# A partner step, two fetches, the spills and the two score lanes put elsewhere in a hybrid decoder layer

## The chip, the cores and the metric

The kernel runs on one core of one Trainium2 chip. The metric is the device time of one execution in microseconds (us); the median of three runs is compared. The engines are TensorE (PE, matmuls), VectorE (DVE), ScalarE (ACT), GpSimd (POOL) and SyncE (SP). SP and POOL here mostly issue DMAs, each in the order of its own program. Every engine works through its program in order and waits at an instruction until the semaphores it needs have been raised.

## The reference

One layer over 256 tokens of width 2048, in float32:

```
h = rmsnorm(x, pre_norm_g);  proj = h @ w_in          # w_in: 2048 x 18448, split into 11 parts
gk  = log_sigmoid(a_lr @ gla_gk_w2 + gla_gk_b) / 16
o_a = gated linear attention(a_q, a_k, a_v, gk)        # 4 heads, keys 256, values 512
y_a = (rmsnorm(o_a) * silu(a_g)) @ w_branch_a
o_b = (softmax(q1 k1) - lam * softmax(q2 k2)) v        # 16 heads, causal, key width 64
y_b = (rmsnorm(o_b) * 0.8 * silu(b_g)) @ w_branch_b
merged = sigmoid(m_a) * y_a + sigmoid(m_b) * y_b
out = x + rmsnorm(merged @ w_out, post_norm_g)
```

## The kernel before

Every weight is read once (some twice) from DRAM as float32 and split into two parts, `hi` and `lo`: ACT copies it rounded (L261), DVE subtracts (L262). A product is then three matmuls, hi x hi, hi x lo and lo x hi. A piece of weights of 128 x 1024 is a *half step*; `take` hands the next one to PE and has the one three places ahead prepared (`AHEAD = 3`; three buffers each for `hi` and `lo`, so ACT waits until PE has let one go).

The work has these stages.

1. The first projections with the values of the linear attention. Beside them, tasks written as generators go forward a piece at each `pump`: `forget_gate` works out the forget gate (absolute value, exponential and logarithm on ACT, last a combination on DVE), `sum_operands` prepares sums of the input's blocks (`s4`, `r1`, `s2`, `r3`).
2. The joint phase. Seven *sets* of 1024 columns are done with seven block products each, by a scheme that needs one product fewer than eight (`PRODUCTS = (1, 3, 5, 6, 2, 7, 4)`). Products 1, 6, 7 and 4 of a set share one PSUM bank `x`: DVE reads it after 6 and after 7 (`gr`, L765 and L773), ACT after 4. So product 4's first matmul waits until DVE has read the bank. A product is two *slots* (t = 0, 1) of two half steps. `phase_steps` mixes the slots with the other projections: behind a slot stands a *partner*, a half step of `others()` (16 matmuls in a `bg` bank), except behind the slots in the list `skip`. There are 14 slots without a partner. In this phase PE's order is the program's (`pinned`).
3. The lanes. `gla_scores` and `gla_out` do the linear attention, two `diff_lane` generators the softmax attention, each in its turn at each `pump`, while the main loop projects the gates, the last heads and `y0`. `q` and `k` of the linear attention were spilled to DRAM and are fetched back (`fetched`) on POOL's queue. A lane's round for a pair of heads is: turned output of the last pair and scores of the first head; scores of the second; turn the first (L1021, evacuated by ACT L1023); weigh the first (L1032 to L1034) and turn the second; weigh the second.
4. `y1`, the merge, the output projection and the norm.

There are eight PSUM banks: four of tag `mm` for main work and four of tag `bg` for everything beside it. Main work and tasks share `take`'s stream of weights. `fetch` keeps its DMA in program order; `spill` leaves it to the scheduler, which may move it among what stands near. Names after `<-` are operands; `raw` is a weight piece as loaded, `a`, `b`, `c` are the sets' weight pieces, which are partly added up by the DMA itself (`accumulate`).

Of the kernel before, what the change touches and what calls it, by code (L numbers as in the profile page):

```python
# [29 lines left out]
SETS = 7  # L30
# [46 lines left out]
def phase_steps():  # L77

    keys = ["v4"] + [f"{name}{hf}{c}" for hf in range(2) for name in ("k", "q") for c in range(4)]
    keys += [f"{name}{g}{c}" for g in EARLY for pair in range(2) for name in ("dq", "dk") for c in (2 * pair, 2 * pair + 1)]  # L80
    other = [(key, r, h) for key in keys for r in range(4 if key == "v4" else 1) for h in range(2)]
    slots = [(s, prod, t) for s in range(SETS) for prod in PRODUCTS for t in range(2)]
    front = [(0, prod, t) for prod in PRODUCTS[:2] for t in range(2)]
    skip = [(SETS - 1, 7, 1), (SETS - 1, 4, 1)] + [(s, prod, 0) for prod in (4, 2) for s in range(SETS - 1, 0, -1)]
    skip = skip[: len(slots) + len(front) - len(other)]
    mixed = []
    for slot in slots:
        mixed += [("set", *slot, h) for h in range(2)]
        for _ in range((slot not in skip) + (slot in front)):
            mixed.append(other.pop(0))  # L90
    return mixed + other
# [3 lines left out]
def hybrid_kernel(ctx: ExitStack, tc, xt, xn, preg, postg, w, w2, gkb, glag, lamv, diffg, ident_d, causal_d, lmask_d, out):  # L95
    nc = tc.nc
    pe, act, dve, pool, sp = nc.tensor, nc.scalar, nc.vector, nc.gpsimd, nc.sync
# [12 lines left out]
    def u(shape, name, dtype=F32):  # L110
        count[0] += 1
        return big.tile(shape, dtype, tag="u", name=f"{name}_{count[0]}")
# [5 lines left out]
    def sm(shape, name, dtype=F32, bufs=2):  # L118
        count[0] += 1
        return pools[0].tile(shape, dtype, tag=name, name=f"{name}_{count[0]}", bufs=bufs)  # L120

    def t2(shape, name):
        count[0] += 1
        return pools[0].tile(shape, F32, tag="t2", name=f"{name}_{count[0]}", bufs=6 if len(pools) == 1 else 12)

    def spill(t, name):
        count[0] += 1
        d = dram.tile(list(t.shape), t.dtype, name=f"{name}_{count[0]}")
        pool.dma_start(d, t)
        return d  # L130

    def fetch(d, name, make, queue=pool):
        t = make(list(d.shape), name, d.dtype)
        tc.keep_in_program_order(queue.dma_start(t, d))
        return t

    def ps(tag):
        count[0] += 1
        return psum.tile([P, 512], F32, tag=tag, name=f"{tag}_{count[0]}")

    def f32(ap):
        return ap.bitcast(F32)
# [370 lines left out]
    def lend(tag, name, dtype=F32):  # L513

        count[0] += 1
        return blocks.tile([P, 8, P], dtype, tag=tag, name=f"{name}_{count[0]}", bufs=1).rearrange("p a t -> p (a t)")

    def forget_gate():
        w2_raw = w2_tile[0]
        yield  # L520
        bank = ps("bg")
        for b in range(2):
            pe.transpose(bank[:, P * b : P * b + P], lr[:, b, :], ident)
        top = t2([P, 512], "lrh").bitcast(F32R)
        lrt = sm([P, S], "lrt", F32R, bufs=1)
        act.activation(top[:, :S], bank[:, :S], AF.Copy)
        for i in (0, 64):
            act.activation(lrt[i : i + 32, :], bank[i : i + 32, :S], AF.Copy)
            r = slice(i + 32, i + 64)
            dve.tensor_tensor(out=lrt[r, :], in0=bank[r, :S], in1=f32(top[r, :S]), op=ALU.subtract)  # L530
        w2_s = lend("s2l", "w2_s", F32R)
        top = lend("r3h", "w2h", F32R)
        r = slice(64, P)
        late = tc.keep_in_program_order
        late(act.activation(w2_s[:64, :], w2_raw[:64, :], AF.Copy))
        late(act.activation(top[r, :], w2_raw[r, :], AF.Copy))
        late(dve.tensor_tensor(out=w2_s[r, :], in0=w2_raw[r, :], in1=f32(top[r, :]), op=ALU.subtract))
        yield
        gp.extend(u([P, 2, 4, P], "gp") for _ in range(2))
        for hf in range(2):  # L540
            for c in range(2):
                bank = ps("bg")
                for i in range(2):
                    ct = 4 * hf + 2 * c + i
                    o = bank[:, S * i : S * i + S]
                    pe.matmul(o, w2_s[:, P * ct : P * ct + P], lrt, start=True, stop=True)
                for i in range(2):
                    ct = 4 * hf + 2 * c + i
                    act.activation(gp[hf][:, :, 2 * c + i, :], bank[:, S * i : S * i + S].rearrange("p (b t) -> p b t", b=2), AF.Identity, bias=gkb_s[:, ct : ct + 1])
            yield  # L550
        e = [lend(tag, "e") for tag in ("r3h", "r3l")]
        z = [t.rearrange("p b c t -> p (b c t)") for t in gp]
        for hf in range(2):
            act.activation(e[hf], z[hf], AF.Abs)
            yield
            act.activation(e[hf], e[hf], AF.Exp, scale=-1.0)
            yield
        for hf in range(2):
            act.activation(e[hf], e[hf], AF.Ln, bias=1.0)
        for hf in range(2):  # L560
            yield
            dve.scalar_tensor_tensor(out=z[hf], in0=z[hf], scalar=0.0, in1=e[hf], op0=ALU.min, op1=ALU.subtract)
        done.add("gate")
# [71 lines left out]
    def late():  # L635
        norm_row()
        yield
        lam()
        yield
# [143 lines left out]
    pinned[0] = True  # L783
    fetched = []
    for step in phase_steps():
        if step == ("set", SETS - 1, 4, 0, 0):
            fetched = [[fetch(ts[name, hf], name, u) for name in ("q", "k")] for hf in range(2)]
        next(sets if step[0] == "set" else rest)
    for gen in (sets, rest):
# [160 lines left out]
    def place(t, d, m, h):  # L950
        tc.keep_in_program_order(sp.dma_start(f32(t[64 * h : 64 * h + 64, m]), d[64 * m : 64 * m + 64]))

    waiting = [(g, pair) for g in range(4) for pair in range(2)]

    def diff_lane(n):
# [11 lines left out]
        def ask():  # L967
            if waiting:
                ahead.append(waiting.pop(0))
                missing.extend(("q", "kh", "kl"))  # L970

        def arrive():
            if not missing or (*ahead[0], "dk") not in heads:
                return
            g, pair = ahead[0]
            part = missing.pop(0)
            for m in range(2):
                for h in range(2):
                    if part == "q":
                        place(q2, heads[g, pair, "dq"][h != m], m, h)  # L980
                    elif part == "kh":
                        place(kh, heads[g, pair, "dk"][0], m, h)
                    elif h == m:
                        place(kl, heads[g, pair, "dk"][1], m, h)
# [24 lines left out]
        def combine(w):  # L1009
            z, prob = w["z"], w["prob"]  # L1010
            c = sm([P, 2], "c", bufs=2)
            dve.reciprocal(out=c, in_=z[:, 2:4])
            dve.scalar_tensor_tensor(out=c, in0=z[:, 0:2], scalar=neg_lam, in1=c, op0=ALU.mult, op1=ALU.mult)
            for b in range(2):
                lo, up = cuts[b]
                dve.scalar_tensor_tensor(out=prob[0][:, lo:up], in0=prob[1][:, lo:up], scalar=c[:, b : b + 1], in1=prob[0][:, lo:up], op0=ALU.mult, op1=ALU.add)
# [46 lines left out]
        while ahead:  # L1063
            late = len(missing)
            while missing:
                arrive()
                yield
            if late:
                yield
            g, pair = ahead.pop()  # L1070
            one, two = (dict(g=g, h=2 * pair + i) for i in range(2))
            if last:
                turned_out(*last)
            last = g, pair
            scores(one)
            if g not in values:
                values[g] = [fetch(gspill[2 * g + 4 + i], name, u, sp) for i, name in enumerate(("dv", "ub"))]
            yield
            combine(one)
            scores(two)  # L1080
            yield
            ask()
            for work in (((turned, one), (combine, two)), ((weighted, one), (turned, two)), ((weighted, two),)):
                arrive()
                for part, w in work:
                    part(w)
                yield
# [6 lines left out]
    for g in range(4):  # L1094
        banks = token_major(f"ag{g}", 512, x_ops, LANES)
        t = u2([P, 2, 512], "ua")
# [62 lines left out]
    for g in range(4):  # L1159
        banks = token_major(f"y1{g}", 512, b_ops, 1 if g else LANES, None if g else settle)  # L1160
        for b in range(2):
            t = gb[g][:, b, :]
# [11 lines left out]
    for b in range(2):  # L1174
        xres.append([])
        for i in range(2):
            t = u([P, 1024], "xres")
# [126 lines left out]
```

## Time and profile before

| | |
|---|---|
| median of 3 runs | 1108.43 us (1108.39 to 1108.62) |
| profiled execution | 1108.06 us, span 1106.3 us, mean granted PE clock 0.997 |
| busy in the span | PE 1092.8 us, DVE 863.2, ACT 680.3, POOL 132.1 |
| DMA | 274.57 MB, mean 248 GB/s |

The span runs from the first to the last instruction; the time includes what lies around it. The profile's rows are start and length in us, engine, line, operation, `out<-in`, shape and count; behind them in brackets the idle time of the engine just before and what ended it. A "busy" PE need not be PE at its peak, since matmuls overlap: one of 512 columns shows 0.39 us, and the next starts after 0.23. So the spacing of starts tells the pace. In lists of waits the columns are total us, times, longest.

The joint phase lies between about 82 and 594 us, the lanes between 594 and 908, `y1` and the merge until about 1014.

### The profile page before, as it was taken

The page shows a single profiled execution, that of the slowest core. Times are in us where ns is not written, and L with a number is a line of the kernel's source. Part 1 is how long each engine was busy: PE and PEld are TensorE (multiplying, and loading weights), DVE is VectorE, ACT ScalarE, POOL GpSimd, SP SyncE. Part 2 cuts the span into 40 slices and gives each one's busy share as a digit, 9 for nine tenths or more (in the row PEclk, how much of TensorE's full clock was granted, in tenths as well). Part 3 has the DMA queues.
Part 4 walks back from the last instruction along what each step waited for, and adds up shares of the span by engine and source line. Part 5 has one row for each costly group of instructions (what it writes and reads, how often), then busy time and mean ns, then how long its engine had stood idle before and what let it go on. Part 6 is the DMA issues. An engine that isn't in the chain of part 4 may idle for free.

```text
span 1106.3 us, 15250 instructions
## 1 busy us (share of the span) xinstructions
PE 1092.8 (99%) x5522; PEld 939.0 (85%) x5522; DVE 863.2 (78%) x1200; ACT 680.3 (61%) x989; POOL 132.1 (12%) x201
## 2 busy tenths in 40 slices
PE   9999999999999999999999999999999999999997
PEld 8999888888888888888887888889888888888886
DVE  7797987979979889798898988668877764655463
ACT  7886766666667667667675555567776653444460
POOL 0201111121021210211212100121110110000000
PEclk9999999999999999999999999999999999999999
DMA  9869979699798897997957654697898666556752
GB/s 346 297 229 326 281 260 312 157 303 300 269 312 218 307 244 248 320 241 276 298 143 276 238 186 153 204 326 262 255 277 270 215 227 211 190 190 220 270 195 76
DMA packets 58268, 274.57 MB, mean 248 GB/s; under 512 B 7824, under 2 KB 9360, under 8 KB 39248
## 3 DMA queue, kind: packets, MB, share of 16 engines
q1 hardware_dynamic: 36192, 184.18, 47.7%
q0 software_dynamic: 20992, 88.09, 28.8%
q10 hardware_dynamic: 1008, 1.32, 0.4%
q8 instruction: 43, 0.70, 0.3%
q14 instruction: 33, 0.27, 0.1%
HBM read 248.40 MB, written 25.17 MB: 247 GB/s over the span
## 4 chain that ended last, share of the span: by engine, by line
PE 97%; DVE 1%; issue 1%; DMA 0%; ACT 0%; DVEq 0%; SPq 0%; POOLq 0%; POOL 0%; ACTq 0%
PE mm L449 65%; PE bg L449 22%; PE bg L437 2%; PE mm L422 2%; PE mm L437 2%; PE bg L862 1%; PE bg L422 1%; PE bg L996 1%; PE bg L997 1%; DMA raw<-in_w_dram 0%; PE bg L1021 0%; PE bg L1034 0%; PE bg L1033 0%; PE bg L1032 0%; PE bg L1153 0%
## 5 line engine op out<-in xcount | busy, mean ns | idle before, releaser
L261 ACT ACTIVATE hi<-raw 128x1024 fp32r<-128x1024 f32 (+3 forms) x275 | 282.6, 1031 | 285.1 <-PE mm L449 175.3
L262 DVE TENSOR_TENSOR lo<-raw,hi 128x1024 fp32r<-128x1024 f32 (+3 forms) x275 | 325.9, 1187 | 147.7 <-ACT hi L261 144.4
L449 PE MATMUL mm<-hi,xs 128*128 128x512 f32 (+1 forms) x848 | 215.6, 389 | 2.2 <-DVE gr L773 1.8
L449 PEld LDWEIGHTS mm<-hi,xs 128*128 128x128 f32 x848 | 157.7, 189 | 29.0 <-issue 2.2
L449 PE MATMUL bg<-xs,hi 128*128 128x512 f32 x640 | 164.9, 390 | 0.0
L262 DVE TENSOR_TENSOR lo<-a,hi 128x1024 fp32r<-128x1024 f32 x112 | 135.2, 1221 | 10.5 <-ACT hi L261 9.3
L449 PEld LDWEIGHTS bg<-xs,hi 128*128 128x128 f32 x640 | 120.4, 188 | 23.3
L261 ACT ACTIVATE hi<-a 128x1024 fp32r<-128x1024 f32 x112 | 118.7, 1060 | 28.2 <-PE mm L449 22.0
L449 PE MATMUL mm<-lo,xs 128*128 128x512 f32 (+1 forms) x424 | 118.5, 385 | 0.1
L449 PEld LDWEIGHTS bg<-xs,lo 128*128 128x128 f32 x640 | 87.3, 191 | 6.2
L449 PEld LDWEIGHTS mm<-lo,xs 128*128 128x128 f32 x424 | 79.7, 189 | 14.9 <-DVE lo L262 0.4
L449 PE MATMUL bg<-xs,lo 128*128 128x256 f32 x640 | 89.3, 283 | 0.0
L262 DVE TENSOR_TENSOR lo<-b,hi 128x1024 fp32r<-128x1024 f32 x56 | 67.5, 1223 | 8.5 <-ACT hi L261 7.6
L261 ACT ACTIVATE hi<-b 128x1024 fp32r<-128x1024 f32 x56 | 59.3, 1061 | 18.5 <-PE mm L449 16.5
L449 PE MATMUL mm<-hi,oah 128*128 128x512 f32 x128 | 50.9, 398 | 0.0
L449 PE MATMUL mm<-hi,obh 128*128 128x512 f32 x128 | 50.4, 394 | 0.0
L449 PE MATMUL mm<-hi,oal 128*128 128x512 f32 x128 | 50.1, 391 | 0.0
L449 PE MATMUL mm<-hi,obl 128*128 128x512 f32 x128 | 49.9, 390 | 0.0
L1007 ACT ACTIVATE prob<-prob,mx,score_scale 128x128 f32<-128x128 f32 x64 | 34.2, 536 | 13.3 <-DVE mx L1002 13.1
L449 PE MATMUL mm<-hi,mh 128*128 128x512 f32 x96 | 37.5, 390 | 0.0
L449 PE MATMUL mm<-hi,ml 128*128 128x512 f32 x96 | 37.4, 390 | 0.0
L198 POOL DMA_DIRECT2D b<-in_w_dram x28 | 24.3, 868 | 108.8 <-DVE a L206 98.4
(288 smaller groups left out, 1874.5 us busy)
## 6 DMA issues: line engine op xcount, KB each, us to landing
raw<-in_w_dram SPq DMA_DIRECT2D x120, 1024.0 KB, 5.6
a<-in_w_dram POOLq DMA_DIRECT2D x28, 512.0 KB, 13.8
c<-in_w_dram SPq DMA_DIRECT2D x28, 512.0 KB, 8.8
b<-in_w_dram POOLq DMA_DIRECT2D x28, 512.0 KB, 7.9
a<-in_w_dram POOLq DMA_DIRECT2D x12, 1024.0 KB, 5.3
b<-in_w_dram POOLq DMA_DIRECT2D x12, 1024.0 KB, 7.9
raw<-in_w_dram SPq DMA_DIRECT2D x14, 832.0 KB, 7.2
dh<-dh POOLq DMA_DIRECT2D x16, 256.0 KB, 4.3
```

Source lines behind the costliest of these rows:

```text
L198: pool.dma_start(chain[s, name, i][:, c], weights(f"set{s}", 2 + i)[0][:, c], accum_op=ALU.add)
L261: act.activation(hi_t[:, a:b], r[:, a:b], AF.Copy)
L262: dve.tensor_tensor(out=lo_t[:, a:b], in0=r[:, a:b], in1=f32(hi_t[:, a:b]), op=ALU.subtract)
L422: i = pe.matmul(out, lhs, rhs, start=first and n == 0, stop=last and n == len(pairs) - 1)
L437: i = pe.matmul(banks[g][b][:, :n], a[part][:, P * b : P * b + P], w[:, n * g : n * g + n], start=first, stop=last)
L449: i = pe.matmul(*args, **kw)
L862: pe.matmul(o, xk[:, P * c : P * c + P], xq.rearrange("p (b c t) -> p b c t", b=2, c=4)[:, :, c, :], start=i == 0, stop=i == 1)
L996: pe.matmul(banks[m][:, lo:up], q2[:, m, i2, t], kh[:, m, i2, :n], start=True, stop=False)
L997: pe.matmul(banks[m][:, lo:up], q2[:, m, i2, t], kl[:, m, i2, :n], start=False, stop=True)
L1007: act.activation(prob[m][:, lo:up], prob[m][:, lo:up], AF.Exp, scale=score_scale[:, b : b + 1], bias=mx[:, i : i + 1], accum_out=z[:, i : ...
```

## The change

Five edits; none adds or takes away arithmetic.

- `skip`: slot (6, 7, 1), the last of product 7 in the last set, gets its partner back, and slot (6, 1, 0), the first of that set, loses its own. All partners of the last set in between move one place later.
- `spill` keeps its DMA in program order.
- `forget_gate`: the two logarithms were issued one after the other; now the first, a `yield`, its combination on DVE, then the second.
- The fetches of `q` and `k` are issued before slot step (6, 7, 1, 1) rather than before (6, 4, 0, 0).
- `diff_lane`: a lane does not begin a pair (turned output, scores) while the other stands between its two scores (`scoring`).

```
-    skip = [(SETS - 1, 7, 1), (SETS - 1, 4, 1)] + [(s, prod, 0) for prod in (4, 2) for s in range(SETS - 1, 0, -1)]
+    skip = [(SETS - 1, 4, 1)] + [(s, prod, 0) for prod in (4, 2, 1) for s in range(SETS - 1, 0, -1)]
     skip = skip[: len(slots) + len(front) - len(other)]
...
-        pool.dma_start(d, t)
+        tc.keep_in_program_order(pool.dma_start(d, t))
...
         for hf in range(2):
             act.activation(e[hf], e[hf], AF.Ln, bias=1.0)
-        for hf in range(2):
             yield
             dve.scalar_tensor_tensor(out=z[hf], in0=z[hf], scalar=0.0, in1=e[hf], op0=ALU.min, op1=ALU.subtract)
...
-        if step == ("set", SETS - 1, 4, 0, 0):
+        if step == ("set", SETS - 1, 7, 1, 1):
             fetched = [[fetch(ts[name, hf], name, u) for name in ("q", "k")] for hf in range(2)]
...
+    scoring = {}
...
+            while scoring.get(1 - n):
+                yield
             g, pair = ahead.pop()
+            scoring[n] = True
...
             scores(two)
             yield
+            scoring[n] = False
```

What this does to the order of the engines' programs, at the three places on which most rests. First PE at the end of set 6, where `mm` is the bank `x`, operands `r3h`/`r3l` are product 7 and `xs` product 4. Before:

```order
L449 MATMUL mm_4814<-hi_5281,r3h 128x512
L449 MATMUL mm_4814<-hi_5281,r3l 128x512
L449 MATMUL mm_4814<-lo_5282,r3h 128x512 x2
L449 MATMUL mm_4814<-hi_5291,xs_79 128x512 x4
L449 MATMUL mm_4814<-lo_5292,xs_79 128x512 x2
```

Now (`bg` is a partner's bank):

```order
L449 MATMUL mm_4813<-lo_5261,r3h 128x512 x2
L449 MATMUL bg_5270<-xs_79,hi_5271 128x512 x2
L449 MATMUL bg_5270<-xs_80,hi_5271 128x512 x2
L449 MATMUL bg_5270<-xs_81,hi_5271 128x512 x2
L449 MATMUL bg_5270<-xs_82,hi_5271 128x512
L449 MATMUL bg_5270<-xs_79,lo_5272 128x256 x2
L449 MATMUL bg_5270<-xs_80,lo_5272 128x256 x2
L449 MATMUL bg_5270<-xs_81,lo_5272 128x256 x2
L449 MATMUL bg_5270<-xs_82,lo_5272 128x256 x2
L449 MATMUL bg_5270<-xs_82,hi_5271 128x512
L449 MATMUL mm_4813<-hi_5291,xs_79 128x512 x4
```

A partner's 16 matmuls now stand between product 7 and product 4. At the start of set 6 the two slots of product 1 follow each other, with no partner between.

Second ACT in the first stage, at the logarithms (L559, `e`), the operand sums (L615, now L614) and the splits. Before:

```order
L559 ACTIVATE e_697<-e_697 128x1024
L559 ACTIVATE e_698<-e_698 128x1024
L615 ACTIVATE s4h<-temp_766 128x1024
L261 ACTIVATE hi_813<-raw_787 128x832
L615 ACTIVATE r1h<-temp_765 128x1024
L261 ACTIVATE hi_836<-raw_787 128x832
```

Now:

```order
L559 ACTIVATE e_697<-e_697 128x1024
L614 ACTIVATE s4h<-temp_766 128x1024
L261 ACTIVATE hi_812<-raw_787 128x832
L559 ACTIVATE e_698<-e_698 128x1024
L614 ACTIVATE r1h<-temp_765 128x1024
L261 ACTIVATE hi_836<-raw_787 128x832
```

One split stands one place sooner; the next one stands where it stood. On DVE the second combination (`gp`) moves in the same way from before the split `lo` of the first of them to behind it.

Third PE in the lanes, at a point where one lane begins a pair. Before (L1034 the weighted values, L1021 turned probabilities, L1051 turned output, L996 and L997 scores, which fill two banks in turn):

```order
L1034 MATMUL bg_7368<-dv_7150,prob_597_7128 128x128
L1021 MATMUL bg_7383<-ident,prob_613_7216 128x128 x3
L1051 MATMUL bg_7388<-ident,ogb_7243 128x128 x4
L996 MATMUL bg_7399<-kh_6616,q_522_6615 128x128
L997 MATMUL bg_7399<-kl_6617,q_522_6615 128x128
L996 MATMUL bg_7400<-kh_6616,q_522_6615 128x128
```

Now, at the piece of main work that has the most tasks beside it (the turned output L1051, into `bg_7588`, stands just ahead of these rows):

```order
L996 MATMUL bg_7601<-kh_6375,q_489_6374 128x128
L997 MATMUL bg_7601<-kl_6376,q_489_6374 128x128
L996 MATMUL bg_7602<-kh_6375,q_489_6374 128x128
L997 MATMUL bg_7602<-kl_6376,q_489_6374 128x128
L996 MATMUL bg_7601<-kh_6375,q_489_6374 128x256
L997 MATMUL bg_7601<-kl_6376,q_489_6374 128x256
L996 MATMUL bg_7602<-kh_6375,q_489_6374 128x256
L997 MATMUL bg_7602<-kl_6376,q_489_6374 128x256
L1032 MATMUL bg_7629<-dv_7207,prob_635_7371 128x128
L1033 MATMUL bg_7629<-dv_7207,prob_635_7371 128x128
L1034 MATMUL bg_7629<-dv_7207,prob_635_7371 128x128
L1021 MATMUL bg_7644<-ident,prob_648_7457 128x128 x3
```

Lane 0 runs one `pump` later against lane 1 than before, so other parts of the two lanes' rounds meet. In the built program `bg_7400` has the bank that `bg_7383` had, and now `bg_7644` has the bank of `bg_7588`. The number of pieces of main work until both lanes are done is the same.

On POOL the four fetches of `q` and `k` now stand ahead of the last `gr` spill and of the last partner's two `dh`/`dl` spills; before they stood behind these. The kept order of the spills moves one early `vh` spill behind a cast of the mask, and one `mgate` spill behind a root and two fetches; nothing else on POOL changes its order by it.

More of the change, by code (lines that the diff above doesn't have):

```diff
@@ L83, in phase_steps @@
     front = [(0, prod, t) for prod in PRODUCTS[:2] for t in range(2)]
-    skip = [(SETS - 1, 7, 1), (SETS - 1, 4, 1)] + [(s, prod, 0) for prod in (4, 2) for s in range(SETS - 1, 0, -1)]
+    skip = [(SETS - 1, 4, 1)] + [(s, prod, 0) for prod in (4, 2, 1) for s in range(SETS - 1, 0, -1)]
     skip = skip[: len(slots) + len(front) - len(other)]
@@ L128, in spill @@
         d = dram.tile(list(t.shape), t.dtype, name=f"{name}_{count[0]}")
-        pool.dma_start(d, t)
+        tc.keep_in_program_order(pool.dma_start(d, t))
         return d
@@ L559, in forget_gate @@
             act.activation(e[hf], e[hf], AF.Ln, bias=1.0)
-        for hf in range(2):
             yield
@@ L785, in hybrid_kernel @@
     for step in phase_steps():
-        if step == ("set", SETS - 1, 4, 0, 0):
+        if step == ("set", SETS - 1, 7, 1, 1):
             fetched = [[fetch(ts[name, hf], name, u) for name in ("q", "k")] for hf in range(2)]
@@ L951, in place @@
         tc.keep_in_program_order(sp.dma_start(f32(t[64 * h : 64 * h + 64, m]), d[64 * m : 64 * m + 64]))
+    scoring = {}
     waiting = [(g, pair) for g in range(4) for pair in range(2)]
@@ L1069, in diff_lane @@
                 yield
+            while scoring.get(1 - n):
+                yield
             g, pair = ahead.pop()
+            scoring[n] = True
             one, two = (dict(g=g, h=2 * pair + i) for i in range(2))
@@ L1081, in diff_lane @@
             yield
+            scoring[n] = False
             ask()
```

## The prediction

> **What bounds the kernel now.** I read the page first, then the waits of TensorE (PE), then the chain that ended last, then the timeline around each place where PE stopped.
>
> ```profile
> PE 1092.8 (99%) x5522; PEld 939.0 (85%) x5522; DVE 863.2 (78%) x1200; ACT 680.3 (61%) x989; POOL 132.1 (12%) x201
> ...
> PE 97%; DVE 1%; issue 1%; DMA 0%; ACT 0%; DVEq 0%; SPq 0%; POOLq 0%; POOL 0%; ACTq 0%
> ```
>
> PE is busy 99% of the span and is 97% of the chain. The change removes no matmul, so it can only win back time in which PE stands still or runs slowly. The waits of PE name the places:
>
> ```profile
> PE mm L449 <- DVE gr L773: 1.8, 1, 1.8
> ...
> PE bg L996 <- ACT prob L1023: 1.1, 3, 0.4
> PE mm L449 <- ACT hi L261: 0.4, 1, 0.4
> ```
>
> These are one stall at the end of the last set, three in the lanes of the softmax attention, one early. The change has a part for each. Before costing them I check what a stall costs beyond its idle time, in PE's timeline around the largest:
>
> ```profile
> 584.73 0.61 PE L449 MATMUL mm<-lo,r3h 128*128 128x512 f32 x2
> 587.18 1.92 PE L449 MATMUL mm<-hi,xs 128*128 128x512 f32 x4 [1.83 <-DVE gr L773]
> ...
> 594.32 1.98 PE L449 MATMUL mm<-hi,xs 128*128 128x512 f32 x8
> ...
> 587.10:590.60 3.50, 3.42 (x9) 0.53 0.38 150
> ...
> 117.13 2.75 PE mm L449 x12
> ...
> 114.36 2.77 PE bg L449 x16
> ```
>
> The first three rows are start, length, instruction; the fourth is a stretch with PE's busy time and then the granted clock, 0.53; the last two are pieces of the chain, a slot of a set (12 matmuls, 2.75 us) and a partner's half step (16 matmuls, 2.77 us). Product 4 of the last set is two slots, so 24 matmuls, 2 x 2.75 = 5.50 us; here it runs from 587.18 to 594.32, 7.14 us. So 1.64 us follow the stall, as half clock. The stall itself: two matmuls at full clock take 2 x 2.75 / 12 = 0.46 us, so the next was due at 584.73 + 0.46 = 585.19 and came at 587.18, 1.99 us late. Together 3.63 us.
>
> **The partner moved: -3.63 us.** Before, product 7's last slot of set 6 has no partner behind it, so PE goes straight to product 4, which writes the bank that VectorE (DVE) must first read:
>
> ```profile
> 585.21 1.22 DVE L262 TENSOR_TENSOR lo<-a,hi 128x1024 fp32r<-128x1024 f32 x1
> 586.34 0.69 DVE L773 TENSOR_TENSOR gr<-mm,p 128x512 f32<-128x512 f32 x1
> ...
> L773 DVE TENSOR_TENSOR gr<-mm,p x7: 685/685/686, 153.4 to 586.3; 128x512 f32<-128x512 f32 x7
> ```
>
> The sum `gr` stands behind a 1.22 us split and ends at 587.03. With the partner, PE has 2.77 us of other matmuls between 585.19 and the need, 587.96: 0.9 us to spare if `gr` ends as before. The seven `gr` of L773 are the sets; the six with a partner there cost PE no wait, since the list of waits has one. Bounds: 0 (a new wait takes it over) to 3.63; I take 3.63, as six of seven cases do.
>
> What pays is slot (6, 1, 0), which loses its partner. No matmul is added, but four split halves (two per slot) now come in 5.50 us. One costs DVE 1.22 us, four 4.88 us, and the partner's evacuations stand beside them; product 2 of six sets and product 4 of five already run so, and the list of waits has none of them. I cost it at nothing; if the cover goes, it is the third rival. The steps after it in set 6 come 2.77 us sooner and their partners 2.77 us later; the DMAs keep their order on SP and POOL.
>
> **`Ln` apart: -0.3 us.** Rows of PE, ScalarE (ACT) and DVE around the early wait:
>
> ```profile
> 68.36 1.68 PE L449 MATMUL mm<-hi,xs 128*128 128x416 f32 x8
> ...
> 70.64 1.67 PE L449 MATMUL mm<-hi,xs 128*128 128x416 f32 x8
> ...
> 73.42 1.78 PE L449 MATMUL mm<-hi,xs 128*128 128x416 f32 x8 [0.36 <-ACT hi L261]
> ...
> 76.12 1.68 PE L449 MATMUL mm<-hi,xs 128*128 128x416 f32 x8
> ...
> 72.41 0.96 ACT L261 ACTIVATE hi<-raw 128x832 fp32r<-128x832 f32 x1
> ...
> 70.78 2.36 DVE L562 SCALAR_TENSOR_TENSOR gp<-gp,e 128x1024 f32<-128x1024 f32 x2
> ...
> 75.13 1.22 DVE L616 TENSOR_TENSOR r1l<-temp,r1h 128x1024 fp32r<-128x1024 f32 x1
> 76.27 1.02 DVE L262 TENSOR_TENSOR lo<-raw,hi 128x832 fp32r<-128x832 f32 x1
> ```
>
> A half tile takes 70.64 - 68.36 = 2.28 us. The next two take 2.78 and 2.70: 0.92 lost. With the second `Ln` behind it, `hi` comes one operation sooner (about 1 us), so the first loss goes. But DVE does the same work up to the `lo` at 76.27: the second `gp` has only moved between two splits. That `lo` ends at 77.29 as before. PE, undisturbed, wants it at 70.64 + 2 x 2.28 + 1.5 = 76.7 (1.5: the `hi` matmuls ahead of it), before at 76.12 + 1.5 = 77.6. It now waits until 77.3 and keeps 0.3. Bounds 0 and 0.92; I take 0.3, since DVE's rows set it.
>
> **Lanes score apart: -0.9 us.** One of the three places:
>
> ```profile
> 800.41 0.38 PE L1032 MATMUL bg<-dv,prob 128*128 128x128 f32 x2
> ...
> 801.08 0.49 PE L1021 MATMUL bg<-ident,prob 128*128 128x128 f32 x3
> 801.40 0.60 PE L1051 MATMUL bg<-ident,ogb 128*128 128x128 f32 x4
> 801.76 0.31 PE L996 MATMUL bg<-kh,q 128*128 128x128 f32 x1
> 801.90 0.28 PE L997 MATMUL bg<-kl,q 128*128 128x128 f32 x1
> 802.54 0.33 PE L996 MATMUL bg<-kh,q 128*128 128x128 f32 x1 [0.36 <-ACT prob L1023]
> 802.70 0.28 PE L997 MATMUL bg<-kl,q 128*128 128x128 f32 x1
> 802.81 0.33 PE L996 MATMUL bg<-kh,q 128*128 128x256 f32 x1
> ...
> 803.34 1.55 PE L449 MATMUL mm<-hi,xs 128*128 128x512 f32 x6
> ...
> 799.44 2.58 DVE L262 TENSOR_TENSOR lo<-raw,hi 128x1024 fp32r<-128x1024 f32 x2
> ...
> 803.82 0.74 DVE L502 SCALAR_TENSOR_TENSOR obl<-bg,diffg_s,obh 128x512 fp32r<-128x512 f32 x1
> ```
>
> Five banks are wanted between two pieces of main work and there are four `bg` banks: the scores' second bank is the one that the turned probabilities (L1021) just filled. From L997 to L996 it is 0.64 us instead of 0.11: 0.53 lost, three times 1.6. In the new order the lanes meet otherwise: turned output, two scores, weighted, turned, again five. By the program's bank assignment the last, the turned probabilities, takes the bank of the turned output of the same piece, twice. Counted from the end of main work (800.41 here): turned output 0.36, the eight score matmuls 803.34 - 801.76 - 0.53 = 1.05, weighted 801.08 - 800.41 = 0.67; PE wants the bank at 2.08. It is free when `obl` has read it: behind the two splits that end at 802.02, 1.61 here, plus 0.74 = 2.35. So about 0.3 lost, twice 0.6; 1.6 - 0.6 gives 1.0, and I take 0.9 since `obl` may start a little later. Bounds: 1.6 (no wait) to below nothing (second rival).
>
> **Fetch sooner, spills in order: 0.** Before, the four fetches issue behind `gr`'s spill:
>
> ```profile
> 589.92 0.55 POOL L134 DMA_DIRECT2D q<-q  x1
> ...
> 598.97 1.22 DVE L822 TENSOR_TENSOR suf<-q,k 128x1024 f32<-128x1024 f32 x1
> ```
>
> The first use follows 9 us later and DVE does not wait for it, so nothing is on PE's path. Now they stand ahead of `gr` on POOL and need only four buffers, the last freed when product 7's first slot is prepared. That keeps the 9 us though PE arrives sooner. What queues behind them, `gr`'s and `dh`'s spills, is not read for 100 us. The spills kept in order move one cast and one spill; no wait of PE is near. If the fetches blocked POOL, the spills would be late and nobody waits.
>
> **The sum.** -3.63 - 0.3 - 0.9 = -4.8 us. The profiled execution took 1108.06 us (span 1106.3 and 1.8 around it), so 1103.2 on that footing; the median of the runs is 1108.43, 0.37 above it: 1103.6. A difference under 0.2% (2.2 us) is what a measurement here cannot tell from none.
>
> **Rivals.** *First: the half clock is not the stall's.* The clock falls at the end of a gap of 1.83 us and lies at half for 3.4 us; other gaps, of 0.36 us, show no fall. If the fall came from something else at that time, it would stay and the partner would save 1.99 us only: -1.99 - 0.3 - 0.9 = -3.2, 1105.2 us. Against it: it starts with the first matmul after the only long gap. Chance 0.07.
>
> [...]
>
> *Second, and slower: the lanes' bank.* If `obl` stands behind two more splits (2.58 us, the row above) at the two new places, PE idles 0.3 + 2.6 = 2.9 us each, and the clock falls as at 587 (1.64 more): 2 x 4.5 = 9.0 lost, less the 3.63 + 0.3 + 1.6 gained: +3.5, 1111.9 us. It decides from a loss of 2.8 us each (5.53 / 2). Against it: DVE's program has `obl` right behind the two splits I counted. Chance 0.04.
>
> *Third: the change does not do what it says, the wait only moves to the start of set 6.* For it: the accumulated loads land late there.
>
> ```profile
> L198 POOL DMA_DIRECT2D a<-in_w_dram x4: 862/877/1222, 524.1 to 530.3; - x4
> ...
> DMA to landing us min/median/max: 5.4/13.3/16.4
> ...
> 548.07 2.12 ACT L261 ACTIVATE hi<-a 128x1024 fp32r<-128x1024 f32 x2
> ...
> 553.54 0.39 PE L449 MATMUL mm<-hi,r1h 128*128 128x512 f32 x1
> ```
>
> The last lands by 530.3 + 16.4 = 546.7. ACT's second split of it starts at about 548.07 + 1.06 = 549.1, 2.4 us later; now it wants to start 2.77 us sooner, 0.4 too early. PE takes that split up at 553.54, 3.4 us after its end at 550.19, and the loads are issued up to 2.77 us sooner too, so nothing should reach PE. If all of them came 5 us later, a stall of 2 us and its half clock take back 3.6: 1107.2 us, no change. Chance 0.11.
>
> **How the numbers follow.** The forecast has 0.78 and its own range is 1102.3 (all three losses gone: 3.63 + 0.92 + 1.6 = 6.15) to 1104.9 (lanes and `Ln` nothing, 3.63 only: 1104.8). The range adds the first rival and reaches a little to the third: 1102.3 to 1106.0, 0.85 by these chances, some 0.8 with sizes that I may have wrong. Under 1106.2 lie the forecast and the first rival: faster 0.85. The third is same, 0.11, the second slower, 0.04.
>
> **What the new profile would show.** Right: no wait of PE on DVE `gr`; product 4 of set 6 in 5.5 us; the clock at 1.00 from 570 to 600; PE's waits in the lanes twice near 0.2 us on DVE `obl` instead of three times 0.36 on ACT; the early wait on `hi` gone and one on DVE `lo` of some 0.5 us near 77; the fetches of `q` and `k` issued near 575. Wrong: a wait of PE between 525 and 560 on splits of `a` or `b`, or at `gr` again, a half-clock stretch anywhere in the middle, or lanes that wait for `obl` over 1 us.

## The result and the profile after

The changed kernel takes 1103.72 us, median of five runs (1103.49 to 1104.39); the kernel before took 1108.43 (five runs, 1107.02 to 1109.15, the three given ahead of the prediction among them). The ratio is 0.9959, 95% interval 0.9945 to 0.9974: faster by 0.26 to 0.55%. The forecast was 1103.6 us, range 1102.3 to 1106.0. So the number was met. But one of its terms holds in full only against runs of before like the profiled one, where the clock falls to 0.50 for 3.41 us, another was too large, and a third, costed at nothing, turned out to be a condition of the first.

The profiled execution of the changed kernel is the run of 1104.39, span 1102.6 us. From its page, engines and chain:

```profile
PE 1090.2 (99%) x5522; PEld 936.9 (85%) x5522; DVE 862.5 (78%) x1200; ACT 680.6 (62%) x989; POOL 132.5 (12%) x201
...
PE 96%; DVE 1%; ACT 1%; issue 1%; DMA 1%; DVEq 0%; SPq 0%; POOLq 0%; POOL 0%; ACTq 0%
```

The shares are within a point of those of before. What changed is in PE's waits (total us, times, longest):

```profile
PE bg L343 <- DVE ones_b L340: 1.6, 1, 1.6
PE bg L437 <- ACT hi L261: 1.6, 1, 1.6
PE mm L449 <- DVE lo L262: 0.4, 1, 0.4
PE bg L1021 <- DVE obl L502: 0.3, 1, 0.3
```

No wait on `gr` is left. The first two lie in the first 9 us; the wait on the first weights (L437) is 1.6 us here and 0.3 in before. PE's timeline at the places of the change:

```profile
78.09 1.02 PE L449 MATMUL mm<-lo,xs 128*128 128x416 f32 x4 [0.41 <-DVE lo L262]
...
582.94 1.75 PE L449 MATMUL bg<-xs,hi 128*128 128x512 f32 x7
...
585.72 1.09 PE L449 MATMUL mm<-hi,xs 128*128 128x512 f32 x4
...
591.18 1.07 PE L449 MATMUL mm<-hi,xs 128*128 128x512 f32 x4
...
785.02 0.55 PE L1021 MATMUL bg<-ident,prob 128*128 128x128 f32 x3 [0.32 <-DVE obl L502]
```

The partner runs from 582.94 to 585.72; product 4 follows without a gap and takes 591.18 - 585.72 = 5.46 us in place of 7.14. The other two rows are the early wait, now on `lo` near 78, and the largest of the lanes' waits, now on `obl`. The granted clock over the end of the joint phase (stretch, length, PE busy, clock, DMA share, GB/s):

```profile
570.00:600.00 30.00, 30.00 (x145) 1.00 0.65 236
```

Setting the main matmuls of both traces beside each other, one by one, gives where the time went: +0.7 us in the first 9 us (a longer wait for the first weights in this execution), -0.27 at the logarithms, -3.6 at the partner, -0.5 in the lanes. Together -3.7, the difference of the spans (1102.6 - 1106.3).

### The profile page after: what moved, and what is told of

It is laid out like the page before. It is cut to its first block, busy times and chain, and to the rows that moved or that the text cites. A ratio compares the mean times of both kernels' runs of the same rounds, so it can differ in the third digit from the quotient of the medians.

```text
span 1102.6 us, 15241 instructions
## 1 busy us (share of the span) xinstructions
PE 1090.2 (99%) x5522; PEld 936.9 (85%) x5522; DVE 862.5 (78%) x1200; ACT 680.6 (62%) x989; POOL 132.5 (12%) x201
## 4 chain that ended last, share of the span: by engine, by line
PE 96%; DVE 1%; ACT 1%; issue 1%; DMA 1%; DVEq 0%; SPq 0%; POOLq 0%; POOL 0%; ACTq 0%
PE mm L449 64%; PE bg L449 22%; PE bg L437 2%; PE mm L422 2%; PE mm L437 2%; PE bg L861 1%; PE bg L422 1%; PE bg L997 1%; PE bg L996 1%; PE bg L1021 1%; DMA raw<-in_w_dram 1%; DVE lo L262 1%; ACT hi L261 0%; PE bg L1157 0%; PE bg L921 0%
```

## The experiments

The theory before them: the partner takes the stall on `gr` and its half clock (3.6), the logarithms 0.3, the lanes 0.5, the rest nothing, each by itself. The rivals: the half clock has another cause; the wait only moves. The experiments ran on two chips (numbers 8 and 3), so a time is compared only with a kernel timed beside it, and terms of less than 1 us are read from the traces by setting the same matmuls beside each other.

### The partner alone

```
-    skip = [(SETS - 1, 7, 1), (SETS - 1, 4, 1)] + [... for prod in (4, 2) ...]
+    skip = [(SETS - 1, 4, 1)] + [... for prod in (4, 2, 1) ...]
```

> The kernel before with the partner's move alone. Theory (the partner takes up the stall on gr and the half clock behind it): no wait of PE on gr, clock 1.00 from 570 to 600 us, product 4 of set 6 in 5.5 us, 3.6 us less than before, near 1104.8 us; the three idle places of PE on ACT prob in the lanes and the early wait on hi stay as before. Rival 1 (the half clock has another cause and stays near 587 to 591): 2.0 us less, near 1106.4. Rival 3 (a new wait on the splits of set 6 takes the gain): within 0.5 us of before.

Measured: 1107.66 us median of ten (1106.76 to 1109.08), before 1106.76 beside it; ratio 1.0010 (1.0000 to 1.0019). The medians show no gain. The stall on `gr` is gone and the clock stays up: against the trace of before the matmuls come 3.56 us sooner across that place. But 30 us later PE waits as it did not before (waits of PE, then its timeline):

```profile
PE bg L855 <- DVE atl L841: 1.2, 1, 1.2
...
PE bg L854 <- ACT ath L840: 0.5, 1, 0.5
```

```profile
619.68 0.50 PE L854 MATMUL bg<-ath,ones_r 128*128 128x512 f32 x1 [0.45 <-ACT ath L840]
621.41 0.50 PE L855 MATMUL bg<-atl,ones_r 128*128 128x512 f32 x1 [1.23 <-DVE atl L841]
```

Start by start, 2.15 us are given back there, and 0.33 more at 840 us in the lanes. So 1.1 us are left against that trace, which has the half clock; against runs of before without it (by their times 11 of the 13 beside this kernel, under 1107.1 us) the partner gains some 2.0 (3.63 - 1.64, an estimate) and gives back 2.5. `ath` and `atl` belong to the first piece of the linear attention, which needs the fetched `q` and `k`. DVE's and POOL's timelines of this kernel:

```profile
592.25 0.68 DVE L671 TENSOR_TENSOR dk<-dk,dh 128x512 f32<-128x512 f32 x1
...
603.75 0.69 DVE L836 TENSOR_TENSOR xq<-xq,q 128x512 f32<-128x512 f32 x1 [5.56 <-DMA q<-q]
```

```profile
593.45 0.54 POOL L129 DMA_DIRECT2D dl<-dk  x1
593.99 0.55 POOL L134 DMA_DIRECT2D q<-q  x1
...
595.65 0.54 POOL L134 DMA_DIRECT2D k<-k  x1
```

And the same in the kernel before:

```profile
588.41 0.69 DVE L671 TENSOR_TENSOR dk<-dk,dh 128x512 f32<-128x512 f32 x1
...
596.30 0.69 DVE L836 TENSOR_TENSOR xq<-xq,q 128x512 f32<-128x512 f32 x1
```

All partners of the last set stand one place later, so the last sum of `dk` starts 3.8 us later (592.25 against 588.41). Their spill stands ahead of the fetches on POOL, so these go out at 593.99 instead of 589.92, just when PE arrives 3.6 us sooner. The transfers also take longer; from issue to landing, before and then here:

```profile
DMA to landing us min/median/max: 5.4/7.1/10.0
```

```profile
DMA to landing us min/median/max: 9.6/11.0/13.3
```

The third rival's idea, that the wait moves, was right for the partner by itself, though at another place. It also shows what the prediction misread: the first use of the fetched data is L836 at 596.30, not L822 at 598.97, and the first transfer landed at about 589.92 + 5.4 = 595.3. The cover was 1 us, not 9, and it rests on the half clock: in the trace of the logarithms alone (below), where product 4 takes 5.56 us (586.92 to 592.48) at a clock of 1.00, DVE already waits 0.76 us for `q`.

### The changed kernel with the old fetch

```
-        if step == ("set", SETS - 1, 7, 1, 1):
+        if step == ("set", SETS - 1, 4, 0, 0):
```

> The changed kernel with the fetches of q and k back at their old step, behind product 7. Theory (there are some 9 us between their landing and the first use, hidden either way): the time of the changed kernel within 0.3 us, 1103.7; the fetches issued some 15 to 20 us later than 567 us; no wait of PE or DVE on q or k. Rival (PE arrives 3.6 us sooner and the fetch is now just late): DVE waits for q near 595 to 600 and PE loses 0.5 to 3 us behind it.

One run of 1107.20 us, 2.8 more than the profiled run of the changed kernel; 1.0 of this is from the first 11 us. The rest is the rival, a little further on. PE's waits and timeline:

```profile
PE mm L449 <- DVE lo L262: 1.4, 2, 1.0
```

```profile
614.70 1.21 PE L449 MATMUL mm<-lo,xs 128*128 128x512 f32 x4 [1.01 <-DVE lo L262]
```

Between 608 and 617 us it falls 1.84 us behind the changed kernel: DVE waits for `k` (1.7 us) until 604.66, its attention work piles up, and a split `lo` behind it comes late. So the sooner fetch is worth about 2 us, by this one trace, and only with the partner moved.

### The fetch and the spills alone

```
-        pool.dma_start(d, t)
+        tc.keep_in_program_order(pool.dma_start(d, t))
...
-        if step == ("set", SETS - 1, 4, 0, 0):
+        if step == ("set", SETS - 1, 7, 1, 1):
```

> The kernel before with the fetches sooner and the spills in program order, nothing else. Theory (hidden): 0.0 us, within 0.3; the four fetches are issued near 570 us rather than 590 to 592, the spill of the last gr stays near 589, and the stall on gr of 1.8 us and its half clock stay. Rival (POOL's fetches delay a spill whose buffer DVE needs, or land on weight loads): a new wait of PE or DVE between 570 and 600 and 0.5 us or more slower.

One run of 1106.40 us, 1106.76 for before. No new wait of PE, as the theory said. But the fetches are not 20 us sooner: they go out at 589.86 to 591.56. Without the partner's move the spill of `dk` still stands ahead of them, and DVE waits 0.6 and 0.2 us for them. The edit pulls the fetches ahead of that spill only when the partners stand one place later. PE's stall is there, 1.83 us at 587.11, and yet the clock stays at 1.00 behind it; the last experiments are about that.

### The partner with the fetch and the spills

Both diffs above together, the logarithms and lanes as before.

> The kernel before with the partner moved, the fetches sooner and the spills in program order; the logarithms and the lanes as before. Theory (the partner's gain needs the sooner fetch: with the old one PE gave back 2.15 us at 619): no wait of PE on gr, no wait of 0.4 us or more between 595 and 625 us, and 2.0 us less than the runs of before without half clock, 3.6 less than those with it: near 1104.5, and no second group of times 1.7 us higher except by the start-up gap. Rival (the fetch is not the cause of the waits near 619): the waits of 0.5 and 1.2 us on ath and atl come again, near 1106.7.

Measured: 1105.17 us median of eight (1104.66 to 1106.62), before 1108.03 beside it; ratio 0.9977 (0.9967 to 0.9987). The list of PE's waits has neither `gr` nor `ath` nor `atl`. Against the trace of before, matmuls are 3.57 us sooner past product 4 and still so at 800 us; 0.2 is given back at 840 us. The six lower times, 1104.66 to 1105.54, lie 0.2 to 1.0 above the 1104.5 foretold. With the kernels above this shows the pair: the partner alone gives its gain back, the fetch alone does nothing, together they keep it. No run moves the partner and the fetch without the kept order of the spills, so what that order adds is not shown.

The fetches then hold nothing up, but the spill of `dk` still does. In the changed kernel `q` and `k` have landed by 578.8, and ACT's first operation for `xq` waits until that spill has landed (ACT's timeline):

```profile
599.29 0.66 ACT L834 ACTIVATE xq<-gp 128x512 f32<-128x512 f32 x1 [5.04 <-DMA dl<-dk]
```

DVE's multiplication by `q` (L836 above, L835 here) follows at 599.98, 3.7 us later than in before, and no wait of PE comes of it.

### The logarithms alone, the lanes alone

```
         for hf in range(2):
             act.activation(e[hf], e[hf], AF.Ln, bias=1.0)
-        for hf in range(2):
             yield
```

> The kernel before with the two logarithms apart alone. Theory (DVE's split lo ends when it did and bounds the second half tile): the wait of PE on hi near 73 goes, a wait on DVE lo of about 0.4 us comes near 78, the main matmuls behind it stand 0.3 us sooner; the stall on gr (1.8 us) and the half clock stay; 0.3 us less. Rival (both losses go): 0.9 us less and no wait on lo. Rival (nothing): 0.0, the waits only change their names.

```
+            while scoring.get(1 - n):
+                yield
             g, pair = ahead.pop()
+            scoring[n] = True
...
             yield
+            scoring[n] = False
```

> The kernel before with the lanes' scoring alone. Theory (the bank is then freed by DVE obl and no longer by ACT): three places with PE idle 0.1 to 0.3 us on obl, about 1.06 us lost there in place of 1.6, so 0.5 us less; stall on gr and half clock as before. Rival (the forecast's sizes): two places, 0.9 us less. Rival (other banks, other meeting without the rest of the change): 0 or a loss, with waits on prob that stay.

The logarithms: one run, 1106.23 us. PE's timeline has the wait foretold:

```profile
77.29 1.03 PE L449 MATMUL mm<-lo,xs 128*128 128x416 f32 x4 [0.41 <-DVE lo L262]
```

The matmuls behind it stand 0.31 us sooner than in before. That is the forecast's term.

The lanes: one run, 1107.77 us, with product 4 of the last set as slow as in the trace of before, 7.20 us (587.29 to 594.49). PE's waits:

```profile
PE mm L449 <- DVE gr L773: 1.8, 1, 1.8
...
PE bg L1022 <- DVE obl L502: 0.6, 2, 0.3
```

From the end of the joint phase to the end, the lanes win 0.33 us; in the changed kernel 0.5 against the trace of before. Both are under the forecast's 0.9.

### Three stalls in the changed kernel

```
-    skip = [(SETS - 1, 4, 1)] + [... for prod in (4, 2, 1) ...]
+    skip = [(SETS - 1, 4, 1)] + [(s, 7, 1) for s in (5, 3, 1)] + [... for prod in (4, 2) ...]
```

> The changed kernel with the partner behind product 7's last slot taken away in three sets in the middle (5, 3 and 1); these partners stand behind other slots of product 1 and 2, so the number of matmuls is the same. Theory (each such place stalls PE about 1.8 us on gr and the clock halves for 3.4 us behind each): three waits of PE on gr of 1.5 to 2 us, three stretches of half clock, 3 x 3.63 = 10.9 us more, near 1114.6. Rival (the stall costs its idle time alone): 3 x 2.0 = 6.0 us more, near 1109.7, clock 1.00 throughout. Rival (the last set is special, its neighbour's work hides the gap elsewhere): 0 to 1 us more.

Measured: ten runs in two groups, four of 1108.31 to 1109.06 and six of 1110.54 to 1110.94. PE's timeline in the profiled one, of the first group:

```profile
231.30 1.16 PE L449 MATMUL mm<-hi,xs 128*128 128x512 f32 x4 [1.29 <-DVE gr L772]
...
376.05 1.16 PE L449 MATMUL mm<-hi,xs 128*128 128x512 f32 x4 [1.29 <-DVE gr L772]
...
518.54 1.17 PE L449 MATMUL mm<-hi,xs 128*128 128x512 f32 x4 [1.83 <-DVE gr L772]
```

Each place without its partner stalls, so the last set is not special. But in this trace none of the three brings half clock (the mean granted clock is 0.999): they cost 5.1 us, start by start, close to the rival's 6.0 and half of the theory's 10.9. The second group of times lies some 2 us higher; the half clock of before cost 1.64, so one such stretch would come near it (an estimate; no trace caught it). So a stall of 1.83 us, the last of the three, does not bring half clock each time. The stretches of the clock show where it came and where not.

### When the clock falls

In the trace of before the granted clock reads 0.50 from 587.32 on for 3.413 us, and again from 1102.73 on, 515.41 us or 151.0 times that length after the first. The rows below are stretches of about that length, cut a whole number of lengths from a fall in the same trace: from and to, length, PE busy (matmuls), granted clock, DMA share, GB/s. Two stretches around the stall in before, and two at its end:

```profile
583.91:587.32 3.41, 1.58 (x8) 1.00 0.00 0
587.32:590.73 3.41, 3.41 (x9) 0.50 0.43 168
1099.32:1102.73 3.41, 0.00 (x0) 1.00 0.65 242
1102.73:1106.14 3.41, 0.00 (x0) 0.50 0.44 161
```

Here 1.83 us idle in a stretch are followed by a clock of 0.50. The lanes alone, the other trace with a slow product 4, has 1.83 us idle ahead of it too. With the logarithms alone the stall is as long, with 1.80 of it in the first stretch:

```profile
585.12:588.54 3.42, 1.62 (x7) 1.00 0.00 0
588.54:591.95 3.41, 3.41 (x17) 1.00 0.89 304
```

The clock stays at 1.00. With the fetch and spills alone the cut goes through the stall, 1.56 of it in the first stretch:

```profile
583.43:586.84 3.41, 1.85 (x9) 1.00 0.04 14
586.84:590.25 3.41, 3.14 (x14) 1.00 0.19 72
```

And the three stalls, the second and the last, with 1.29 and 1.50 idle:

```profile
373.68:377.09 3.41, 2.12 (x10) 1.00 0.97 329
377.09:380.51 3.42, 3.42 (x17) 1.00 1.04 434
517.04:520.45 3.41, 1.91 (x8) 1.00 1.00 382
520.45:523.87 3.42, 3.42 (x17) 1.00 1.02 398
```

The end of the program gives two more cases. First the long stall (the experiment below), then the three stalls: the last stretch with matmuls, and the next.

```profile
1102.46:1105.88 3.42, 1.43 (x12) 1.00 0.77 293
1105.88:1109.29 3.41, 0.00 (x0) 0.50 0.66 251
```

```profile
1097.31:1100.72 3.41, 1.62 (x14) 1.00 0.72 275
1100.72:1104.13 3.41, 0.00 (x0) 1.00 0.66 248
```

1.99 us idle, and 0.50 in the next; 1.79 idle, and 1.00 in the next.

So among the stretches at full clock that are shown here with the next one, those with 1.83, 1.99, 2.01 (the last experiment) and 3.41 us idle have 0.50 behind them, and those with 1.29 to 1.80 have 1.00. Idle times rest on modelled ends of matmuls, so 1.80 and 1.83 are hardly apart, and these are a few stretches. Of the five stalls of 1.83 us looked at here, two had half clock behind them (before, and by the 7.20 us of product 4 the lanes alone) and three had not (the logarithms alone, the fetch and spills alone, the last of the three stalls); what decides between them was not shown. The times of before allow both cases but don't show them: its 45 runs lie either at 1106.2 to 1107.1 or at 1107.7 to 1109.5, 22 and 23 of them. Yet the second group has 2 of 13 on chip 8 and 17 of 27 on chip 3, a difference that stays open, and some of it is the start's (below): versions without the stall have a group some 1.3 to 2.2 us higher too, 8 of their 27 runs. The trace that the prediction worked from has the fall, and the three times shown belong to the second group.

The test: a longer stall at the same place.

```
-                            with tc.high_priority(offset=100):
-                                dve.tensor_tensor(out=halves["r"][:, 1, :], in0=x, in1=kept[5], op=ALU.add)
+                            for _ in range(5 if s == SETS - 1 else 1):
+                                with tc.high_priority(offset=100):
+                                    dve.tensor_tensor(out=halves["r"][:, 1, :], in0=x, in1=kept[5], op=ALU.add)
```

> The kernel before with DVE's sum gr of the last set's product 7 issued five times in place of once (four repeats with the same result, each 0.60 us on from the last), so that the stall of PE on gr is 4.2 us long in place of 1.83. [...] Rival (the fall is a matter of chance for each stall, half of them as before): half of the runs near 1108.9, half near 1110.5.

The size was missed: the repeats came to stand between other work of DVE and the stall is 6.42 us, not 4.2. The times are 1113.54 to 1113.80 in four runs; before, beside it, spreads over 1106.45 to 1109.52. The stretches:

```profile
583.64:587.05 3.41, 1.96 (x9) 1.00 0.03 10
587.05:590.46 3.41, 0.00 (x0) 1.00 0.20 77
590.46:593.88 3.42, 1.86 (x5) 0.50 0.20 77
593.88:597.29 3.41, 3.41 (x10) 0.50 0.86 264
597.29:600.70 3.41, 3.41 (x16) 1.00 1.00 399
```

1.45 us idle, and 1.00 in the next; 3.41 idle, and 0.50 in the next; 1.56 idle in a stretch that is at 0.50 already, and 0.50 in the next. Since the stall grew past the plan, a whole stretch has no matmul here, and stalls between 1.83 and 6.42 us were not run. The run speaks against the rival of chance. The sum closes: 6.42 - 1.83 = 4.6 more idle time and 5.27 us of matmuls at a clock of 0.50, taken as 2.6 lost (an estimate: half of 5.27), over the lower group of before (median 1106.7) give 1113.9. Four runs in one group don't exclude chance by themselves (half of them would fall by chance in 1 case of 16), but no run lies near 1111.3, where the sum without half clock is.

### A version that beats both

```
+            for _ in range(0 if hf else 3):
+                yield
...
-            if last:
-                turned_out(*last)
-            last = g, pair
...
             scores(two)
             yield
             scoring[n] = False
+            if last:
+                turned_out(*last)
+            last = g, pair
```

The second logarithm waits three pieces longer, and a lane's turned output stands behind its two scores, so at most four banks are wanted between two pieces of main work.

> The changed kernel with two more edits: the second logarithm and its combination three pieces later, so that DVE's split lo does not stand behind other work near 77 us, and in a lane's round the turned output behind the two scores instead of ahead of them, so that at most four banks are wanted between two pieces of main work. Theory: PE's wait on lo near 78 goes (0.53 us) and the three places on obl in the lanes go (1.06 us): 1.6 us less than the changed kernel, near 1102.2. Rival (the next operation is as late, and the lanes meet at another bank): 0 to 0.5 us less. Rival (the later turned output delays the lanes' end and the start of y1): slower by 0.5 us or more, with a gap near 908.

> The changed kernel once more, on the same chip as the kernels beside it, to compare with e9_partner_fetch (0.8 us less than that by the logarithms, 0.27, and the lanes, 0.5) and e7_better (some 1.6 us more than that). Near 1103.7; the runs spread under 1 us, but for a start-up gap long enough to bring a half clock (1.7 us more).

> The improved kernel once more beside the changed one on one chip. Theory: 1.6 us under the changed kernel (0.53 of the wait on lo, 1.06 of the three on obl). Rival (the earlier 2 us between them were two chips and two start-up gaps): within 0.5 us of it.

First time: 1101.72 us median of five, ratio to before 0.9943 (0.9929 to 0.9956). Beside each other on one chip: this version 1101.43, 1101.56, 1103.42 and 1103.48, median 1102.49, ratio 0.9953 (0.9936 to 0.9970); the changed kernel 1103.37 to 1103.97 in three runs and 1105.40 and 1105.56 in two, median 1103.97, ratio 0.9969 (0.9956 to 0.9982). The changed kernel's trace stands 0.31 us (logarithms) and 0.7 (lanes) ahead of the one with partner and fetch alone; 0.2 of the 0.7 is one longer wait in the lanes of that kernel. The intervals of the two overlap, so the times beside each other don't show the difference; the traces tell more. This version's waits of PE, all of them:

```profile
PE bg L343 <- DVE ones_b L340: 1.6, 1, 1.6
PE bg L437 <- ACT hi L261: 0.8, 1, 0.8
```

Both lie in the first 9 us. Start by start it wins 0.65 us at the `lo` wait and 1.6 in the lanes, 2.25 together, 0.6 more than foretold. It has the wait on `obl` in none of the three places. The two groups some 2 us apart come from the start, at least in the one trace that caught it (PE's stretches in the first run of this version):

```profile
4.57:7.98 3.41, 1.40 (x6) 1.00 1.03 363
7.98:11.39 3.41, 3.27 (x9) 0.50 1.04 430
```

The wait for the first weights was 1.9 us there, 2.01 us idle in the stretch, and the clock is 0.50 in the next. This start stays in all versions; it was not worked on.

## Why the prediction was right, and where not

- **The partner, -3.63.** Right for the trace that it was worked from: -3.6 there, the stall and the half clock both. The first rival had the half clock wrong: it begins behind the stall in before, and with the stall gone the clock is 1.00 from 570 to 600. But its size of gain holds wherever before has no half clock: there the partner saves about 2 us (1.99). The prediction took one trace's fall as certain. The forecast of the time did not suffer, since a before without half clock is lower by the same 1.6. And the gain stays only because the fetch moved too, which the prediction did not know.
- **The logarithms, -0.3.** Right: -0.27 in the changed kernel and -0.31 alone, bounded by `lo` as worked out.
- **The lanes, -0.9.** Too large: -0.5. The step that failed is the count of places, two with 0.3 lost at each. The turned probabilities wait for `obl` at three places. The two foretold, at 821 and 857, idle 0.12 and 0.13 us, and the start comes 0.40 us after the one before in place of 0.11, so 0.3 is lost at each, as worked out. The one left out, at 785, has two main matmuls ahead of it; I took these for enough cover, but it idles 0.32 us and starts 0.71 us after the one before in place of 0.23. So 1.06 us of the 1.6 stay lost, and 0.5 are won.
- **The fetch, 0.** The number is right for the edit alone, the working is wrong. "The first use follows 9 us later" took L822; L836 reads `q` at 596.30, 1 us after the landing. Most of the 9 us was the transfer itself, 5.4 for the first of the four. With the partner moved the fetch had to move too, and the edit is worth about 2 us. The issue was foretold for 575 and came at 567.56, ahead of `dk`'s spill. That nobody waits for a late spill is wrong too: ACT waits 5.04 us for `dk`'s, though PE does not feel it.
- **The wait moves to the start of set 6** (third rival, 0.11): no wait of PE there, in any run with the partner moved. The lanes' bank (second rival): waits of 0.3 us at most, not 2.9.
- **The sum.** -3.6 - 0.27 - 0.5 = -4.4 in place of -4.8. The trace of after shows -3.7 because its start was 0.7 longer; the median lies 0.7 below that execution, and so 0.1 above the forecast. So close a hit is luck: the 0.4 that the lanes fell short is made up by the 0.37 added for the median of before, and single runs spread by more through the start. Against runs of before without half clock the sum is -2.0 - 0.27 - 0.5 = -2.8; the lower groups beside each other on chip 3 have medians of 1106.71 and 1103.94, 2.8 apart.

## What to carry to other kernels

Look at what a removed stall was hiding: a transfer's cover is measured from its landing to the first reader of any of its data, and a stall ahead of it is part of that cover (here 595.3 to 596.30, 1 us, with the stall still there). When work moves in a queue, ask what the next issue in that queue now stands behind; here one spill of `dk` decided whether four fetches went out near 567 us or near 594. A single trace shows one case: behind a stall of 1.83 us the clock fell in two traces here and stayed at 1.00 in three. So see whether the times of the kernel come in groups before booking its cost as certain.

## What was not expected of the hardware

Behind the same stall of 1.83 us the clock was 0.50 for 3.41 us in before and 1.00 with the logarithms alone; the stall cost 3.6 us in the one and 2.0 in the other. The two stalls of 1.29 us were not followed by half clock. The fetches' time to landing rose from 5.4 to 10.0 us to 9.6 to 13.3 when they were issued 4 us later. From the first issue to the last landing (589.92 to 601.6) all DMAs together moved 339 GB/s in before; what makes the fetches slower was not tested.
